# The second product of a squared-ReLU MLP: three of its four rounds by seven half-size products in place of eight

## The chip, the core and the metric

One Trainium2 chip, one of its cores. The metric is device time of one execution in microseconds (us). TensorE (PE) multiplies, VectorE (DVE) and ScalarE (ACT) do the elementwise work, GpSimd (POOL) some small parts, SyncE (SP) starts the transfers. The runs of the kernel before took 2602.18, 2602.62 and 2603.87 us.

## The reference

Four residual layers on 512 tokens of 1024 channels, float32. Layer i has a token mixer (retention in layers 0 and 3, a Conformer convolution in layer 1, a short gated convolution in layer 2) and then an MLP with 4096 hidden channels; each sublayer stands between two RMS norms.

```python
def squared_relu_mlp(x, w1, w2):
    return jnp.square(jax.nn.relu(x @ w1)) @ w2

    for i in range(DEPTH):
        ...
        x = x + rms_norm(h, norm_g[i, 1])
        h = squared_relu_mlp(rms_norm(x, norm_g[i, 2]), mlp_w1[i], mlp_w2[i])
        x = x + rms_norm(h, norm_g[i, 3])
```

## The kernel before, in words

Every float32 operand of a product is split into two float32r parts, the first part by ACT and the rest by DVE, and each product is three (`mm3`, lines 273 to 278): high by high, high by low, low by high. Weights come as pieces of 128x1024 (512 KB) in the order in which they are used (`piece_list`, line 64). `load` (line 214) starts the transfer of the next piece into one of two raw buffers, `fetch_hi` (L243) and `fetch_lo` (L250) split it into `whi` and `wlo`, of which there are `W_BUFS` = 8 of each. `settle` (line 260) splits one piece for each that has been used up, so pieces stand split some steps ahead.

All engines' orders are the order of the program: each engine takes its instructions one after the other. Only the conformer's part is ordered by a list schedule (`Plan`, line 128) with its own estimates of costs; `AHEAD` there is the number of pieces of the following product that it splits beforehand.

A sublayer begins with `first_four` (line 301): its first four channel tiles, of 128 channels, in two halves of the tokens, while the last token blocks are still normed, transposed (L393) and placed in `xin` (L324, L325). Then `tile` (line 292) makes one channel tile after the other, for all 512 tokens in one PSUM bank: 24 products of 512 columns (L286, L287, L289).

The MLP runs in four rounds q. In each, eight channel tiles of the first product come out of PSUM by relu (ACT, L1149), its square (DVE, L1150; ACT for the first part, L1151) and the second part (DVE, L1152) into two tiles `hid` of 4x512 columns. Then `out_round` (line 402) multiplies the 1024 hidden channels by eight pieces of the second weight matrix, token-major: two column halves, four pieces each, four token blocks in four banks (L276 to L278). The banks are copied to `f` (ACT, L417, first round) or added to it (DVE, L419). The last round is `out_final` (line 451), which also does the norm after the sublayer (`post_norm`, `add`, L368, L376), the norm before the next (`pre_sum`, `pre_norm`, L382), and the transposes. The residual stream `x` stays in SBUF through the MLP; only ahead of layer 3 it is parked in DRAM, since retention uses its place.

Of the kernel before, what the change touches and what calls it, by code (L numbers as in the profile page):

```python
# [16 lines left out]
P = 128  # L17
# [8 lines left out]
W_BUFS = 8  # L26
# [3 lines left out]
# the depthwise convolution: its channel tiles that run on the tensor engine as products of two  # L30
# token phases with pieces of 8 taps, and how many taps of each other tile the Pool engine adds up
# [5 lines left out]
AHEAD = 8  # L37
# [9 lines left out]
# columns of the per-partition parameter array  # L47
# [16 lines left out]
def piece_list():  # L64
    """The weight pieces in the order in which the kernel consumes them."""
# [10 lines left out]
    for layer in LAYERS:  # L76
# [44 lines left out]
        for q in range(4):  # L121
            for ft in range(8):
                ws("mlp_w1", layer, 8 * q + ft)
            ts("mlp_w2", layer, range(4 * q, 4 * q + 4))
# [3 lines left out]
class Plan:  # L128
    """Orders jobs of several engines by a list schedule and issues them in that order."""
# [10 lines left out]
    def run(self):  # L140
# [12 lines left out]
        while todo:  # L153
# [10 lines left out]
            # a more important job that is about to be ready goes first  # L164
# [12 lines left out]
class Trunk:  # L177
    def __init__(self, tc, wall, x_in, pos, norm_g, small, bpw2, decay, out):
# [3 lines left out]
        self.pieces = piece_list()  # L182
        self.issued = self.from_wall = self.loaded = self.used = self.owed = 0
# [30 lines left out]
    def load(self):  # L214
        """Starts the transfer of the next piece."""
# [4 lines left out]
        if self.pieces[i][0] == "phase":  # L220
            return self.load()
# [8 lines left out]
    def fetch_hi(self):  # L230
        """The first float32r part of the next piece."""
# [7 lines left out]
        if kind == "phase":  # L239
# [5 lines left out]
    def fetch_lo(self, i):  # L245
        """The second part."""
        nc = self.nc
        hi, lo = self.ready[i]
        if self.pieces[i][0] != "phase":
            nc.vector.tensor_sub(lo, self.raws.pop(i), hi.bitcast(F32))  # L250
            if i > 3:
                self.load()

# [6 lines left out]
    def settle(self, most=99):  # L260
        """Splits a piece for each one that has been used up."""
        while self.owed and most and not self.planned:
# [29 lines left out]
    def tile(self):  # L292
        """The next channel tile of a product, for all tokens."""
# [33 lines left out]
    def high(self, hi, lo, val):  # L327
        """The first part now, the second with the next call or with flush()."""
# [21 lines left out]
    def begin_boundary(self, post, pre):  # L350
        """Tiles for the end of one sublayer and the start of the next."""
# [50 lines left out]
    def out_round(self, slots, first):  # L402
        """One round of 8 contraction tiles that is not the last; adds into f."""
# [31 lines left out]
    def ts_part(self, banks, piece, slots, kp, late=False):  # L435
        """late: the second parts of slots come later than the first."""
# [137 lines left out]
    def retention(self, layer, first):  # L574
# [14 lines left out]

        def rope(banks, which):  # L590
            b1, b2 = banks
            for half in range(2):
# [9 lines left out]
                # the last block of keys meets only its own queries: it stays float32  # L602
# [167 lines left out]
    def newton(self, v, r0, t, eps):  # L770
        """-2/sqrt(v + eps) by one Newton step from the table's value r0; t holds its square."""
# [6 lines left out]
    def build_phases(self):  # L778
        """The matrices of the convolution's taps for POLY, in float32r parts, to DRAM.

        Rows (s, ch), columns (k, p, ch'): the tap 2k + s - p of channel ch, where ch = ch'."""
        nc = self.nc
        n = 64 * len(POLY)
        taps = self.mix.tile([P, 2, n], F32R, tag="st", bufs=1, name="taps")
        mask = self.mix.tile([P, 64], F32, tag="slast", bufs=1, name="mask")
# [65 lines left out]
        # the order of the tensor engine  # L851
# [282 lines left out]
    def mlp(self, layer, first):  # L1134
        nc = self.nc

        src = self.tiles(first)
        for q in range(4):
            slots = []
            for ft in range(8):  # L1140
                bank = next(src)
                if layer + 1 < DEPTH and mixer_of(layer + 1) == 1:
                    for _ in range(2 if ft == 7 else 1):
# [256 lines left out]
```

## Time and profile before

| | before |
|---|---|
| median of three runs | 2602.62 us (2602.18 to 2603.87) |
| profiled execution | span 2600.4 us from its first to its last instruction; the start and end around it have no time of their own on the page |
| instructions | 30770 |
| DVE, ACT, POOL busy | 1344.6 us (52%), 1011.5 us (39%), 213.1 us (8%) |
| HBM read, written | 256.88 MB, 12.58 MB |

The profile is taken in one execution of the program. "Busy" adds the lengths of an engine's instructions, overlaps counted once; for PE, products overlap in the pipe, so the spacing of their starts, not their length, tells how fast they go. Idle time of an engine counts only where another waits for it.

### The profile page before, as it was taken

How to read it: one execution, taken by the hardware profiler on the slowest of the kernel's cores; microseconds unless marked ns; L12 is line 12 of the kernel's file. 1: busy time of each engine (PE TensorE's matmuls, PEld its weight loads, DVE VectorE, ACT ScalarE, POOL GpSimd, SP SyncE). 2: the span in 40 equal slices, each digit the busy share in tenths (PEclk: the TensorE clock that was granted, in tenths of full speed). 3: DMA queues.
4: the chain of work that ended last, by engine and by line, in shares of the span. 5: the costliest groups of instructions: out<-in, count | busy, mean ns of one | idle time of the engine just before them, and what ended most of it. 6: DMA issues, size and time to landing. Idle time of an engine off the chain costs nothing. (4 is left out here: it accounts for less than half of the span.)

```text
span 2600.4 us, 30770 instructions
## 1 busy us (share of the span) xinstructions
PE 2577.7 (99%) x12461; PEld 2175.4 (84%) x12461; DVE 1344.6 (52%) x1615; ACT 1011.5 (39%) x1485; POOL 213.1 (8%) x248
## 2 busy tenths in 40 slices
PE   9999999999999999999999999999999999999998
PEld 8888888888888788888888888888888888888887
DVE  7654347345458973343464453343746534634433
ACT  4543445323236653322332343223444344433321
POOL 1000001000018710000010100000100000100000
PEclk9999999999999999999999999999999999999999
DMA  4333233334323433222322232223322323222221
GB/s 157 101 98 105 81 130 111 116 124 134 120 79 124 162 114 114 97 91 97 105 98 98 81 122 97 97 98 114 118 85 86 101 81 124 96 97 97 98 98 57
DMA packets 79838, 273.10 MB, mean 105 GB/s; under 512 B 8912, under 2 KB 10704, under 8 KB 79696
## 3 DMA queue, kind: packets, MB, share of 16 engines
q1 hardware_dynamic: 79696, 271.13, 31.0%
q8 instruction: 98, 1.61, 0.3%
q14 instruction: 44, 0.36, 0.0%
HBM read 256.88 MB, written 12.58 MB: 104 GB/s over the span
## 5 line engine op out<-in xcount | busy, mean ns | idle before, releaser
L250 DVE TENSOR_TENSOR wlo<-raw,whi 128x1024 fp32r<-128x1024 f32 x436 | 537.1, 1234 | 671.0 <-ACT whi L243 655.1
L286 PE MATMUL bank<-xin,whi 128*128 128x512 f32 (+1 forms) x2112 | 752.4, 365 | 0.2 <-ACT xin L324 0.2
L287 PE MATMUL bank<-xin,wlo 128*128 128x512 f32 (+1 forms) x2112 | 749.5, 363 | 0.0
L243 ACT ACTIVATE whi<-raw 128x1024 fp32r<-128x1024 f32 x436 | 457.7, 1053 | 627.3 <-PE bank L278 524.5
L289 PE MATMUL bank<-xin,whi 128*128 128x512 f32 (+1 forms) x2112 | 472.9, 364 | 3.7 <-DVE xin L325 3.7
L286 PEld LDWEIGHTS bank<-xin,whi 128*128 128x128 f32 x2112 | 398.3, 189 | 62.7 <-ACT xin L324 0.5
L287 PEld LDWEIGHTS bank<-xin,wlo 128*128 128x128 f32 x2112 | 398.5, 189 | 62.3
L289 PEld LDWEIGHTS bank<-xin,whi 128*128 128x128 f32 x2112 | 368.4, 189 | 67.7 <-DVE xin L325 5.4
L276 PE MATMUL bank<-whi,hid 128*128 128x512 f32 (+1 forms) x1032 | 400.3, 388 | 0.0
L278 PE MATMUL bank<-whi,hid 128*128 128x512 f32 (+1 forms) x1032 | 399.8, 387 | 0.0
L277 PE MATMUL bank<-wlo,hid 128*128 128x512 f32 (+1 forms) x1032 | 399.8, 387 | 0.0
L1150 DVE SCALAR_TENSOR_TENSOR tmp<-bank,tmp 128x512 f32<-128x512 f32 x128 | 88.4, 691 | 282.1 <-ACT tmp L1149 282.1
L278 PEld LDWEIGHTS bank<-whi,hid 128*128 128x128 f32 x1032 | 193.8, 188 | 39.7
L276 PEld LDWEIGHTS bank<-whi,hid 128*128 128x128 f32 x1032 | 193.8, 188 | 39.6
L277 PEld LDWEIGHTS bank<-wlo,hid 128*128 128x128 f32 x1032 | 193.8, 188 | 39.2
L1149 ACT ACTIVATE tmp<-bank 128x512 f32<-128x512 f32 x128 | 76.4, 597 | 374.1 <-PE bank L289 374.1
L344 POOL TENSOR_SCALAR tiny<-tiny,tiny 128x1 f32<-128x1 f32 x32 | 52.4, 1637 | 1550.9 <-ACT tmp L363 1549.7
L1010 POOL TENSOR_TENSOR pbuf<-pbuf 128x512 f32<-128x512 f32 x69 | 99.6, 1458 | 17.3 <-DMA raw<-wall 14.1
L276 PE MATMUL bank<-whi,y 128*128 128x512 f32 x256 | 99.9, 390 | 0.0
L278 PE MATMUL bank<-whi,y 128*128 128x512 f32 x256 | 99.6, 389 | 0.0
L276 PE MATMUL bank<-whi,xin 128*128 128x512 f32 x256 | 99.6, 389 | 0.0
L277 PE MATMUL bank<-wlo,xin 128*128 128x512 f32 x256 | 99.6, 389 | 0.0
(180 smaller groups left out, 2522.8 us busy)
## 6 DMA issues: line engine op xcount, KB each, us to landing
raw<-wall SPq DMA_DIRECT2D x436, 512.0 KB, 3.2
bnd<-norm_g SPq DMA_DIRECT2D x16, 512.0 KB, 6.4
phase<-tmp SPq DMA_DIRECT2D x32, 256.0 KB, 3.9
x<-x_in SPq DMA_DIRECT2D x8, 512.0 KB, 6.2
whi<-phase SPq DMA_DIRECT2D x8, 512.0 KB, 6.8
wlo<-phase SPq DMA_DIRECT2D x8, 512.0 KB, 8.3
early<-wall SPq DMA_DIRECT2D x4, 512.0 KB, 8.8
dec<-decay SPq DMA_DIRECT2D x8, 256.0 KB, 2.7
```

The costliest lines, as they stand in the source:

```text
L243: nc.scalar.activation(hi, self.raws[i], AF.Copy)
L250: nc.vector.tensor_sub(lo, self.raws.pop(i), hi.bitcast(F32))
L276: nc.tensor.matmul(out, ah, bh, start=start, stop=False)
L277: nc.tensor.matmul(out, ah, bl, start=False, stop=False)
L278: nc.tensor.matmul(out, al, bh, start=False, stop=stop)
L286: self.nc.tensor.matmul(out, wh[:, c], x, start=kt == 0, stop=False)
L287: self.nc.tensor.matmul(out, wl[:, c], x, start=False, stop=False)
L289: self.nc.tensor.matmul(out, wh[:, kt * P:(kt + 1) * P], self.xin[:, 1, kt, t0:t1], start=False, stop=kt == 7)
L344: nc.gpsimd.tensor_scalar(ms, parts[0], parts[1], EPS, op0=ALU.add, op1=ALU.add)
L1010: nc.gpsimd.tensor_tensor(accs[c], accs[c], pbuf[:, slot, :], op=ALU.add)
L1149: nc.scalar.activation(r, bank, AF.Relu)
L1150: nc.vector.scalar_tensor_tensor(s, bank, 0.0, r, op0=ALU.max, op1=ALU.mult)
```

## The change

In the first three rounds of each MLP (`FAST` = 3) the second product is done by Strassen's algorithm in the form of Winograd. The 512 tokens, the 1024 hidden channels and the 1024 output channels are halved each, so that there are four blocks of hidden values (two token halves `near[0]` and `near[1]`, the four even tiles `a` and the four odd tiles `b` in the order `PAIRED`) and four blocks of weights. Seven sums or differences of blocks ("forms") are multiplied, in the order `FORMS`, in place of eight products of blocks, and `takers` says to which quarters of `f` each form's result is added or from which it is subtracted.

What follows from this in the code:

- The hidden values: relu and square on ACT, then per pair of tiles four additions or subtractions of 256 columns on DVE (`s14`, `s23`), and splits into the tiles `own`, `far`, `mid`, `end`. `mid` takes the place of the residual `x`, which each mixer's `out_final` now stores to DRAM (`park`), and which is read back in the fourth round.
- The weights: the eight pieces of a round are loaded unsplit into eight blocks `blk` (`load_block`); a form's two pieces are made of them in place by `combine` (DVE) for forms 5, 6, 7 and 4, and split like a piece (14 for 8). In round 0 the eight loads start together after the MLP's first tile; in rounds 1 and 2 one with each piece of the first product.
- The sums: a form has two banks; each goes to one or two quarters of `f` (20 additions of 512 columns per round for 8, in round 0 eight of them as copies on ACT). `fast_end` makes two late sums in the fourth round.
- Room: `W_BUFS` and `AHEAD` are 7 for 8. `first_four` first splits pieces until four are ready. The rotary tables are stored to DRAM in layer 0 and read back in layer 3.

PE's list has 10,301 rows before and 10,013 now. The core of the diff:

```diff
-W_BUFS = 8
+W_BUFS = 7
-AHEAD = 8
+AHEAD = 7
+FAST = 3
+FORMS = (1, 2, 5, 6, 3, 7, 4)
+PAIRED = (0, 4, 1, 5, 2, 6, 3, 7)
...
     def fetch_lo(self, i):
...
+        if kind == "fast":
+            self.combine(*self.pieces[i + 1])
+            nc.vector.tensor_sub(lo, self.form_of(c, n), hi.bitcast(F32))
...
+            if name == "mlp_w1" and 1 <= c // 8 < FAST:
+                self.load_block(idx, c // 8, PAIRED.index(c % 8))
...
+        a, b = {5: ((0, 1), (0, 0)), 6: ((1, 1), (0, 0)), 7: ((1, 1), (0, 1)), 4: ((1, 0), (0, 0))}[form]
+        self.nc.vector.tensor_sub(self.form_of(form, g), self.blk[(g, *a)], self.blk[(g, *b)])
...
     def first_four(self, start):
+        self.settle(4 - len(self.ready))
         pieces = self.use(4)
...
+        def hidden():
+            bank = next(src)
+            s = self.tmp()
+            nc.scalar.activation(s, bank, AF.Relu)
+            nc.scalar.activation(s, s, AF.Square)
+            return s
...
+        for q in range(FAST):
...
+            for i in range(4):
+                a = hidden()
+                if q == 0 and i == 0:
...
+                    for n in range(8):
+                        self.load_block(layer, 0, n)
+                self.split(own[:, 0, i, near[0]], own[:, 1, i, near[0]], a[:, near[0]])
+                build(False)
+                b = hidden()
+                self.split(far[:, 0, i, :], far[:, 1, i, :], b)
...
+                nc.vector.tensor_add(s14[:, near[0]], a[:, near[1]], b[:, near[1]])
+                nc.vector.tensor_sub(s23[:, near[0]], s14[:, near[0]], a[:, near[0]])
+                nc.vector.tensor_sub(s23[:, near[1]], a[:, near[0]], a[:, near[1]])
+                nc.vector.tensor_sub(s14[:, near[1]], b[:, near[0]], s23[:, near[0]])
+                self.split(own[:, 0, i, near[1]], own[:, 1, i, near[1]], s14[:, near[0]])
+                self.split(mid[:, 0, i, :], mid[:, 1, i, :], s23)
+                self.split(end[:, 0, i, :], end[:, 1, i, :], s14[:, near[1]])
+                build(i == 3)
...
+    def fast_round(self, left, first):
...
+        takers = {1: ((0, 0, 1), (1, 1, 1)), 2: ((0, 0, 1),), 5: ((1, 1, 1), (1, 0, -1)), 6: ((1, 1, 1),),
+                  3: ((0, 1, 1),), 7: ((1, 1, 1), (0, 1, -1)), 4: ((1, 0, 1),)}
+        for form in FORMS:
+            banks = [self.bank(), self.bank()]
+            tile, t0 = left[form]
+            for g in range(2):
+                self.settle()
+                (piece,) = self.use()
+                for j in range(2):
+                    k = 2 * g + j
+                    for n, bank in enumerate(banks):
+                        c = slice(t0 + n * P, t0 + (n + 1) * P)
+                        self.mm3(bank, (tile[:, 0, k, c], tile[:, 1, k, c]), self.rhs(piece, j), k == 0, k == 3)
+                self.owed += 1
+            for n, bank in enumerate(banks):
+                for m, d, sign in takers[form]:
...
+            def park(b):
+                nc.sync.dma_start(self.x_park[b], self.x[:, b, :])
...
-                    first = self.out_final(slots, mode, None)
+                first = self.out_final(slots, mode, park)
```

DVE's order at the boundary of layer 0's mixer and MLP, before: the add of token block 3, a piece's second part, the placing of block 2, the norm of block 3, and the placing of block 3.

```order
L376 SCALAR_TENSOR_TENSOR x_2941<-f_2047,tiny_3280,x_2941 128x1024
L250 TENSOR_TENSOR wlo_3336<-raw_3048,whi_3335 128x1024
L325 TENSOR_TENSOR xin_2949<-bank_3325,xin_2949 128x4x128
L325 TENSOR_TENSOR xin_2949<-bank_3330,xin_2949 128x4x128
L382 SCALAR_TENSOR_TENSOR bnd_2946<-x_2941,tiny_3348,bnd_2946 128x1024
L250 TENSOR_TENSOR wlo_3353<-raw_3078,whi_3352 128x1024
L325 TENSOR_TENSOR xin_2949<-bank_3406,xin_2949 128x4x128
L325 TENSOR_TENSOR xin_2949<-bank_3411,xin_2949 128x4x128
L250 TENSOR_TENSOR wlo_3433<-raw_3339,whi_3432 128x1024
```

The same place after the change (L428 is the add, L282 the second part of a piece, L377 the placing, L434 the norm):

```order
L428 SCALAR_TENSOR_TENSOR x_2939<-f_2045,tiny_3282,x_2939 128x1024
L282 TENSOR_TENSOR wlo_3294<-raw_3047,whi_3293 128x1024
L282 TENSOR_TENSOR wlo_3350<-raw_3077,whi_3349 128x1024
L377 TENSOR_TENSOR xin_2948<-bank_3339,xin_2948 128x4x128
L377 TENSOR_TENSOR xin_2948<-bank_3344,xin_2948 128x4x128
L434 SCALAR_TENSOR_TENSOR bnd_2945<-x_2939,tiny_3362,bnd_2945 128x1024
L282 TENSOR_TENSOR wlo_3367<-raw_3297,whi_3366 128x1024
L377 TENSOR_TENSOR xin_2948<-bank_3420,xin_2948 128x4x128
L377 TENSOR_TENSOR xin_2948<-bank_3425,xin_2948 128x4x128
L282 TENSOR_TENSOR wlo_3447<-raw_3353,whi_3446 128x1024
```

One more second part of a piece (`wlo`) stands between the add of block 3 and the placing of block 2, ahead of the norm of block 3 (`bnd`).

DVE's order in the second product, round 1 of layer 0, before: second parts of pieces, and after four of them the additions of four banks into `f`.

```order
L250 TENSOR_TENSOR wlo_4355<-raw_4271,whi_4354 128x1024
L250 TENSOR_TENSOR wlo_4385<-raw_4311,whi_4384 128x1024
L250 TENSOR_TENSOR wlo_4415<-raw_4358,whi_4414 128x1024
L250 TENSOR_TENSOR wlo_4445<-raw_4388,whi_4444 128x1024
L419 TENSOR_TENSOR f_3764<-f_3764,bank_4350 128x512
L419 TENSOR_TENSOR f_3764<-f_3764,bank_4351 128x512
L419 TENSOR_TENSOR f_3764<-f_3764,bank_4352 128x512
L419 TENSOR_TENSOR f_3764<-f_3764,bank_4353 128x512
```

Round 1 of layer 0 after the change, from the first form on (`blk` are weight blocks; L303 is `combine`, L280 the second part of a form's piece):

```order
L1287 TENSOR_TENSOR f_3816<-f_3816,bank_4462 128x512 x2
L1287 TENSOR_TENSOR f_3816<-f_3816,bank_4463 128x512 x2
L280 TENSOR_TENSOR wlo_4504<-blk_3483,whi_4503 128x1024
L303 TENSOR_TENSOR blk_3482<-blk_3483,blk_3482 128x1024
L280 TENSOR_TENSOR wlo_4520<-blk_3479,whi_4519 128x1024
L1287 TENSOR_TENSOR f_3816<-f_3816,bank_4501 128x512
L1287 TENSOR_TENSOR f_3816<-f_3816,bank_4502 128x512
L303 TENSOR_TENSOR blk_3479<-blk_3479 128x1024
L280 TENSOR_TENSOR wlo_4541<-blk_3482,whi_4540 128x1024
L303 TENSOR_TENSOR blk_3481<-blk_3481,blk_3480 128x1024
L280 TENSOR_TENSOR wlo_4558<-blk_3479,whi_4557 128x1024
L1287 TENSOR_TENSOR f_3816<-f_3816,bank_4538 128x512
```

Between two forms' additions stand two second parts and up to two combinations, where eight additions and eight second parts made up the round before.

## Rows read from the trace of the kernel before

**Rows 1.** The page: busy time of each engine; granted clock in 40 slices.

```profile
PE 2577.7 (99%) x12461; PEld 2175.4 (84%) x12461; DVE 1344.6 (52%) x1615; ACT 1011.5 (39%) x1485; POOL 213.1 (8%) x248
...
PEclk9999999999999999999999999999999999999999
```

**Rows 2.** Stretches of layer 3's MLP: length, busy us (instructions) by engine, clock, DMA.

```profile
2331.78:2375.30 43.52, 43.52 (x193) 36.04 (x193) 19.50 (x22) 16.81 (x23) 0.00 (x0) 1.00 0.28 91
2375.30:2418.82 43.52, 43.52 (x193) 36.04 (x193) 15.64 (x17) 9.61 (x10) 0.00 (x0) 1.00 0.30 103
```

**Rows 3.** Groups of instructions: line, engine, tiles, shapes, count | busy us, mean ns | idle.

```profile
L276 PE MATMUL bank<-whi,hid 128*128 128x512 f32 x1016 | 395.7, 390 | 0.0
L250 DVE TENSOR_TENSOR wlo<-raw,whi 128x1024 fp32r<-128x1024 f32 x436 | 537.1, 1234 | 671.0 <-ACT whi L243 655.1
L243 ACT ACTIVATE whi<-raw 128x1024 fp32r<-128x1024 f32 x436 | 457.7, 1053 | 627.3 <-PE bank L278 524.5 <-DMA raw<-wall 65.1 <-PE bank L289 29.8
L1151 ACT ACTIVATE hid<-tmp 128x512 fp32r<-128x512 f32 x128 | 81.0, 633 | 4.1
L419 DVE TENSOR_TENSOR f<-f,bank 128x512 f32<-128x512 f32 x64 | 42.5, 684 | 19.8 <-PE bank L278 19.8
L337 DVE TENSOR_TENSOR st<-tmp,st 128x256 fp32r<-128x256 f32 x8 | 3.4, 426 | 0.2
```

**Rows 4.** Timeline of DVE, layer 3's MLP: start us, length us, instruction [idle before].

```profile
2257.52 1.23 DVE L250 TENSOR_TENSOR wlo<-raw,whi 128x1024 fp32r<-128x1024 f32 x1 [1.10 <-ACT whi L243]
2258.66 0.69 DVE L1150 SCALAR_TENSOR_TENSOR tmp<-bank,tmp 128x512 f32<-128x512 f32 x1
2259.45 0.69 DVE L1152 TENSOR_TENSOR hid<-tmp,hid 128x512 fp32r<-128x512 f32 x1
...
2393.89 1.28 DVE L419 TENSOR_TENSOR f<-f,bank 128x512 f32<-128x512 f32 x2
```

**Rows 5.** Timeline of DVE, boundary of layer 3's mixer and MLP.

```profile
2247.12 1.28 DVE L376 SCALAR_TENSOR_TENSOR x<-f,tiny,x 128x1024 f32<-128x1024 f32 x1 [0.77 <-POOL tiny L347]
...
2250.66 1.27 DVE L382 SCALAR_TENSOR_TENSOR bnd<-x,tiny,bnd 128x1024 f32<-128x1024 f32 x1
...
2253.76 1.29 DVE L325 TENSOR_TENSOR xin<-bank,xin 128x512 fp32r<-128x512 f32 x2 [0.69 <-ACT xin L324]
```

**Rows 6.** Timeline of ACT, the same boundary.

```profile
2253.13 1.09 ACT L324 ACTIVATE xin<-bank 128x512 fp32r<-128x512 f32 x2 [2.58 <-PE bank L393]
```

**Rows 7.** Timeline of PE, first transposes of all; then the same boundary.

```profile
9.53 2.29 PE L393 MATMUL bank<-ident,bnd 128*128 128x128 f32 x16 [1.40 <-DVE bnd L382]
...
2250.57 0.64 PE L289 MATMUL bank<-xin,whi 128*128 128x256 f32 x4
...
2252.01 0.64 PE L289 MATMUL bank<-xin,whi 128*128 128x256 f32 x4
2252.49 1.03 PE L393 MATMUL bank<-ident,bnd 128*128 128x128 f32 x8
```

**Rows 8.** PE's waits: line waited for: us in total, times, longest us.

```profile
PE bank L914 <- DVE conv L990: 4.4, 2, 3.5
PE bank L393 <- DVE bnd L382: 4.1, 3, 1.6
PE bank L289 <- DVE xin L325: 3.7, 8, 0.9
```

**Rows 9.** DMA issues: count, KB, median us to landing; a stretch of the start (last: GB/s).

```profile
raw<-wall SPq DMA_DIRECT2D x436, 512.0 KB, 3.2
early<-wall SPq DMA_DIRECT2D x4, 512.0 KB, 8.8
park<-x SPq DMA_DIRECT2D x4, 512.0 KB, 2.7
...
2.10:16.00 13.90, 11.77 (x82) 10.90 (x81) 7.68 (x9) 8.47 (x14) 2.93 (x6) 1.00 0.97 370
```

More of the change, by code (lines that the diff above doesn't have):

```diff
@@ L121, in piece_list, with blocks, wall_list @@
         for q in range(4):
-            for ft in range(8):
+            for ft in PAIRED if q < FAST else range(8):
                 ws("mlp_w1", layer, 8 * q + ft)
-            ts("mlp_w2", layer, range(4 * q, 4 * q + 4))
+            if q < FAST:
+                out.extend(("fast", layer, q, form, g) for form in FORMS for g in range(2))
+            else:
+                ts("mlp_w2", layer, range(4 * q, 4 * q + 4))
+    return out
+def blocks(q):
+    return [((g, r, c), (4 * q + 2 * r + g, c)) for r, c in ((0, 0), (1, 0), (0, 1), (1, 1)) for g in range(2)]
+def wall_list():
+    out = [p for p in piece_list() if p[0] in ("ws", "ts")]
+    for layer in LAYERS:
+        for q in range(FAST):
+            out += [("ts", "mlp_w2", layer, *where) for _, where in blocks(q)]
     return out
@@ L219, in load @@
         self.issued += 1
-        if self.pieces[i][0] == "phase":
+        if self.pieces[i][0] not in ("ws", "ts"):
             return self.load()
@@ L260, in settle @@
     def settle(self, most=99):
-        while self.owed and most and not self.planned:
+        while self.owed and most > 0 and not self.planned:
             self.fetch()
@@ L588, in retention @@
         nc.vector.tensor_copy(ones, one)
+        if layer:
+            self.cos, self.sin = (rp.tile([P, S], F32, tag=n, bufs=1, name=self.nm(n)) for n in ("cos", "sin"))
+            for there, here in zip(self.angles, (self.cos, self.sin)):
+                nc.sync.dma_start(here, there)
         def rope(banks, which):
@@ L1137, in mlp @@
         src = self.tiles(first)
[L1138 to L1143, printed above, removed]
-                        next(self.building, None)
-                if ft % 4 == 0:
-                    slots.append(self.big.tile([P, 2, 4, S], F32R, tag="h", bufs=2, name=self.nm("hid")))
-                hh, hl = slots[-1][:, 0, ft % 4, :], slots[-1][:, 1, ft % 4, :]
-                r, s = self.tmp(), self.tmp()
-                nc.scalar.activation(r, bank, AF.Relu)
-                nc.vector.scalar_tensor_tensor(s, bank, 0.0, r, op0=ALU.max, op1=ALU.mult)
-                nc.scalar.activation(hh, r, AF.Square)
-                nc.vector.tensor_sub(hl, s, hh.bitcast(F32))
-            if q < 3:
-                self.out_round(slots, q == 0)
@@ new lines, in mlp @@
+        slots = []
+        for ft in range(8):
+            a = hidden()
+            if ft % 4 == 0:
+                slots.append(self.big.tile([P, 2, 4, S], F32R, tag="h", bufs=2, name=self.nm("hid")))
+            self.split(slots[-1][:, 0, ft % 4, :], slots[-1][:, 1, ft % 4, :], a)
+            if ft == 0:
+                self.x = self.big.tile([P, 4, D], F32, tag="x", name=self.nm("x"))
+            if 0 < ft < 5:
+                nc.sync.dma_start(self.x[:, ft - 1, :], self.x_park[ft - 1])
+            if ft in (3, 5):
+                self.fast_end(ft // 2 - 1)
+            build(ft == 7)
@@ new lines, in mlp @@
+        return slots, "add"
+    def fast_round(self, left, first):
+        nc = self.nc
+        if first:
+            self.f = self.big.tile([P, 4, D], F32, tag="f", name=self.nm("f"))
+        takers = {1: ((0, 0, 1), (1, 1, 1)), 2: ((0, 0, 1),), 5: ((1, 1, 1), (1, 0, -1)), 6: ((1, 1, 1),),
+                  3: ((0, 1, 1),), 7: ((1, 1, 1), (0, 1, -1)), 4: ((1, 0, 1),)}
+        seen = set()
+        for form in FORMS:
[12 more added lines that the diff above has]
+                for m, d, sign in takers[form]:
+                    f = self.f[:, 2 * m + n, d * 512:(d + 1) * 512]
+                    if first and (m, d) not in seen:
+                        nc.scalar.activation(f, bank, AF.Copy, scale=float(sign))
+                    elif sign > 0:
+                        nc.vector.tensor_add(f, f, bank)
+                    else:
+                        nc.vector.tensor_sub(f, f, bank)
+            seen.update((m, d) for m, d, _ in takers[form])
@@ L1218, in rotary @@
         nc.scalar.activation(self.cos, t, AF.Sin, scale=-1.0, bias=self.half_pi)
+        for there, here in zip(self.angles, (self.cos, self.sin)):
+            nc.sync.dma_start(there, here)
         yield
@@ L1235, in build @@
             self.x_park = [dram.tile([P, D], F32, name=f"park{b}") for b in range(4)]
+            self.angles = [dram.tile([P, S], F32, name=f"angle{n}") for n in range(2)]
             self.neg_half = self.const(-0.5, "neg_half")
@@ L1294, in begin @@
                 banks = [next(f)]
-                for _ in range(3):
+                for _ in range(W_BUFS - 5):
                     next(turn)
                     self.fetch()
-                next(turn)
+                for _ in range(9 - W_BUFS):
+                    next(turn)
                 next(turn)
@@ L1316, in build @@
                 self.begin_boundary((layer, 3), self.next_pre)
-                store = None
-                if not last and mixer_of(layer + 1) == 0:
-                    store = lambda b: nc.sync.dma_start(self.x_park[b], self.x[:, b, :])
-                first = self.out_final(slots, mode, store)
+                back = not last and mixer_of(layer + 1) == 0
+                first = self.out_final(slots, mode, park if back else None)
 def decay_tables():
@@ L1345, in tile_of @@
         return t[i] if form == "ws" else t[i, c]
-    pieces = [p for p in piece_list() if p[0] != "phase"]
+    pieces = wall_list()
     wall = np.empty((len(pieces), P, D), np.float32)
```

55 lines of the change are left out of this document (47 added, 8 removed).

## The prediction

> **What bounds the kernel now.** I read the page's busy times first: the tensor engine (PE) is busy for 2577.7 of 2600.4 us, at its higher clock level throughout (2.4 GHz, granted clock in tenths 9 in all 40 slices) [rows 1]. So the time is the number of products times their spacing, plus some 23 us in which PE has nothing to do. Next I cut one MLP into stretches: eight tiles of the first product take 43.52 us, and so does one old round of the second product, and in both PE is busy to the last hundredth [rows 2]. 192 products of 512 columns stand in each (the count of 193 includes one cut by the edge): 43.52 / 192 = 0.2267 us from one to the next, 5.44 us for the 24 of one tile. The 390 ns that the groups give for one product [rows 3] is its length in the pipe, not its spacing, and isn't used. VectorE (DVE) is busy 19.50 us in the first of these stretches and 15.64 us in the second, ScalarE (ACT) 16.81 and 9.61 [rows 2]: both have more than half of the time free. PE's own waits are short and lie at the sublayer boundaries and in the conformer [rows 8].
>
> **The products.** An old round is 2 column halves x 4 pieces x 4 token blocks x 2 x 3 = 192 products. A new one is 7 forms x 2 pieces x 2 x 2 token blocks x 3 = 168, of the same 128x128 weights and 512 columns. That is 24 fewer, 24 x 0.2267 = 5.44 us; with 3 rounds in each of 4 layers 288 products and **65.3 us**. PE's order confirms the count: 10,301 rows before, 10,013 now. The products sit in stretches where PE never waits, so each one left out shortens the path, if the other engines keep up.
>
> By the Trainium skill (TensorE: Matmul & The Clock Gate, Part 1) a warm product starts N / 2.4 GHz + 2.5 ns after the one before, 215.7 ns for 512 columns. The rows say 226.7 ns, so the trace doesn't agree; by the page's figure the gain would be 288 x 0.2157 = 62.1 us and the time about 3 us above my forecast.
>
> **DVE in a new round.** The spacing counts here, not the length: a subtraction of 1024 columns starts at 2257.52 and the next instruction at 2258.66, 1.14 us; one that needs the result before it takes 0.79 us at 512 columns (2258.66 to 2259.45); two additions out of PSUM take 1.28 us together, so 1.28 - 0.68 = 0.60 us each [rows 3, 4]. For 256 columns I take the mean of one, 0.43 us [rows 3], and 0.10 us for each being dependent (0.79 - 0.69): 0.53 us. A round with its eight tiles then has on DVE: 8 + 14 second parts of weight pieces and 8 combinations of weight blocks, 30 x 1.14 = 34.2; 20 additions into f, 20 x 0.60 = 12.0; and for each of four pairs of tiles 7 of 256 columns and 2 of 512, 7 x 0.53 + 2 x 0.60 = 4.9, together 19.6. Sum 65.8 us, against 8 x 5.44 + 38.1 = 81.6 us of PE. In layer 0 the matrices for the convolution add nine instructions of 512 columns, about 0.69 us each, 72.0 us. ACT has 22 first parts at 1.05 = 23.1 [rows 3], 16 passes over banks and squares at 0.63 = 10.1, and five splits per pair, at most 0.63 each, 12.6: 45.8 us. So neither becomes the bound on average.
>
> The densest place is the first four forms: 8 second parts, 5 combinations, 12 additions, 13 x 1.14 + 12 x 0.60 = 22.0 us beside 4 x 5.44 = 21.8 us of PE. DVE enters it late, by the chain behind the last tile (relu and square 1.26, then a first part, a second part, four adds, the remaining parts: some 5.5 us), and leaves it some 5.7 us late. What may it be late? A piece is split six pieces ahead of its use (7 buffers), and a piece is now 12 products, 2.72 us: 16.3 us. In PSUM, four forms of two banks each fill the 8 banks, so an addition has three forms, 16.3 us, too. Margin about 10 us: I cost the work on DVE and ACT at nothing, hidden by PE's products. If this cover is gone, a round costs what DVE's sum exceeds 81.6 by.
>
> **Block loads.** Rounds 1 and 2 load one block per first-product tile, the bytes of before at their old pace. Round 0 sends eight at once, 4 MB, behind the first tile of the MLP. At the start, 13.9 us moved 370 GB/s [rows 9], so 4 MB need some 11 us. The first form's product is eight tiles, more than 33 us, away. ACT and DVE may stand for some us behind such a load (in layer 0 also behind a small load for the taps that is queued after the blocks); PE then has its pieces and banks for several tiles. Cost nothing.
>
> **Boundaries.** This is where the 7 buffers cost. Before, four pieces were split when the next sublayer began; now three are, and the fourth is split after the add of token block 3 and before the placing of block 2. DVE's row shows what stands behind: add at 2247.12, one split, two placings, the norm of block 3 from 2250.66 to 2251.93 [rows 5]; PE's transposes of that block began at 2252.49 [rows 7]. Slack 0.56 us; the extra 1.14 us pushes the norm to 2253.07, and PE waits 0.58 us. At two boundaries PE already waits there (of three waits, together 4.1 us, the longest 1.6, one of 1.40 is at the start) [rows 7, 8]: there the whole 1.14 counts. Seven boundaries: 5 x 0.58 + 2 x 1.14 = 5.2 us.
> The second thing there: two raw buffers serve the first two splits, and now a third split, ahead of block 3's placing on ACT, needs a transfer that starts only when the first is done, about 2249.5. It lands 3.2 us later (median) [rows 9], 2252.7, splits until 2253.8; ACT's placing stood at 2253.13 after 2.58 us of idle [rows 6] and now begins about 2253.8. PE's work between, transposes (about 1.0) and one eighth (1.44) [rows 7], runs to about 2255.5, so placing until 2254.9 is in time. At the four boundaries with a parked residual, the store of block 3 (2.7 us to land) runs just ahead of that transfer and can make it later: between 0 and 1.5 us each; I take 0.25, because the slack of 0.6 us swallows most: 1.0 us. Sum for boundaries **6.2 us**, with 0 and 14 us as the ends (14: 7 x 1.14 + 4 x 1.5).
>
> **The rest.** The reload of the residual is in the last quarter, ahead of its use by tiles: nothing. Reloaded rotary tables: two transfers of 256 KB at the start of layer 3, and two stores in layer 0 that SP issues once the sine is there; raw loads behind them have a lead of pieces: nothing. In the conformer the planner orders the same work with one buffer fewer. PE's order there has the same products, DVE's taps move by a place or two; PE waits 4.4 us for DVE there [rows 8], which may grow or shrink by one second part either way, -1 to +2 us; I take 0.
>
> **Sum.** 2600.4 - 65.3 + 6.2 = 2541.3 for the span. The median of the three runs, 2602.62, lies 2.2 us above the span; I keep these: **2543.5 us**. What the measurement can tell from no change is about 0.2%, 5 us.
>
> **Rivals.**
> *DVE runs late in the rounds (chance 0.12).* For it: in rounds of layer 0, 72.0 of 81.6 us, and each second part needs ACT's first part; at boundaries such partners let DVE idle by 0.6 to 0.7 us (0.69 before the placing, [rows 5]). If each of the 22 second parts paid 0.6 us, +13 us: 79 us in most layers, 85 in layer 0. Then layer 0 loses 3 x 3.5 us and the densest stretches of the other nine rounds perhaps 1 us: 20 us, 2563. Against it: first parts run well ahead, since ACT has little else to do in a round.
> *The boundaries cost nothing (0.06)*: 2537. The norm's slack could be larger where PE arrives later.
> *Slower than before (0.03).* The eight block loads of round 0 come one after the other at the 8.8 us that transfers took to land when many were queued at the start [rows 9]. Eight are 70.4 us, and combining and splitting 3.5 more, 73.9; PE asks for the eighth block's first piece after 8 tiles and 7 pieces less the part of the first tile, about 33 + 19 = 52 us. Wait 22 us in each of 4 layers, 88 us: 2543.5 + 88 = 2631. It turns to slower when a layer waits over 59 / 4 = 15 us, that is over 8 us a block. Against: 8.8 us is the time in a queue with others, and the window of 370 GB/s shows 1.4 us per block.
> That the change does less than it says can't be: the products are counted.
>
> **How the numbers follow.** Forecast 0.79, its own range 2537 to 2552 (boundaries 0 to 14). DVE late 0.12, no boundary cost 0.06, slower 0.03. The range of 8 in 10 takes the forecast's ends and reaches to the DVE rival: 2536 to 2562. Faster by over 0.2% holds in all but the last and small part of the DVE case: 0.95; within 0.2% 0.02; slower 0.03.
>
> **What would show it.** Products in a new round: 168 in 38.1 us with PE busy throughout; PE's span of an MLP shorter by 16.3 us. PE waiting for the norm of block 3 (transposes) some 0.6 us more at each boundary, and for nothing in the rounds. DVE busy 60 to 70 us of each 81.6. The forecast is wrong if PE's list of waits names weight pieces or banks inside the rounds, if products come slower than 0.2267 us there, or if ACT's wait for block loads reaches PE in round 0.

## The result, and the profile after

The changed kernel takes 2545.99 us (median; 2543.64 to 2547.59) where the kernel before takes 2602.49 in the same session (2602.18 to 2603.87): 0.9781 of it, 95% interval 0.9768 to 0.9795. The forecast was 2543.5 in a range of 2536 to 2562: the direction and nearly all of the size are right, and the time is 2.5 us above it. The profiled execution has a span of 2544.1 us, 56.3 less than before.

The page of the changed kernel, busy times and granted clock:

```profile
PE 2516.4 (99%) x12173; PEld 2124.6 (84%) x12173; DVE 1652.9 (65%) x2151; ACT 1210.3 (48%) x1829; POOL 218.4 (9%) x248
...
PEclk9999999999999999999999999999999999999999
```

Against [rows 1] PE has exactly 288 products fewer, but is busy 61.3 us less, not 65.3; its idle time (span less busy) rose from 22.7 to 27.7 us. So 56.3 = 65.3 - 5.0 of new idle time - 4.0 of longer busy time: products at the lower clock (some 3.4 us more than before, below), and the ends of products ahead of new stops. A 512-column product that nothing follows counts as busy for its whole 0.39 us, where the next one would have started after 0.23. DVE has 308 us more, ACT 199.

Windows of layer 3's second round, as [rows 2]: first the eight tiles, then the seven forms.

```profile
2286.37:2329.89 43.52, 43.52 (x194) 36.04 (x193) 30.11 (x46) 25.76 (x40) 0.00 (x0) 1.00 0.33 122
2329.89:2367.97 38.08, 38.08 (x170) 31.53 (x169) 31.17 (x39) 15.40 (x18) 0.00 (x0) 1.00 0.20 72
```

The round is 5.44 us shorter and PE is busy to the hundredth. 38.08 us for 168 products is 0.2267 us each (the two more counted are cut by the edges). The forms take 38.08 us in all twelve rounds of the changed kernel but the first of layer 0 (38.69).

Where PE waits, as [rows 8] (L445 was L393, L971 was L914, L340 was L289):

```profile
PE bank L445 <- DVE bnd L434: 8.2, 8, 2.5
PE bank L971 <- DVE conv L1047: 4.3, 1, 4.3
PE bank L340 <- DVE xin L377: 3.2, 8, 0.9
PE bank L337 <- ACT xin L376: 2.3, 2, 2.0
PE bank L237 <- POOL ident masks.py:199: 1.3, 1, 1.3
PE bank L498 <- ACT z L1144: 0.9, 1, 0.9
PE bank L329 <- DVE own L377: 0.3, 1, 0.3
```

Two lines matter. The transposes (L445) wait at all seven boundaries and at the start, 4.1 us more in all (3.5 at the boundaries; the wait at the start is anything from 0.7 to 1.9 us in the kernels of this study); and a wait of 2.0 us for a placing (L337 behind ACT) is new. The first two boundaries' transposes:

```profile
424.09 1.06 PE L445 MATMUL bank<-ident,bnd 128*128 128x128 f32 x8 [0.56 <-DVE bnd L434]
764.65 1.06 PE L445 MATMUL bank<-ident,bnd 128*128 128x128 f32 x8 [2.49 <-DVE bnd L434]
```

In the rounds PE waits 0.3 us in the whole program (`own`, layer 0), and the round there is 0.6 us longer than the others.

The new wait stands at the boundary between layer 2's MLP and layer 3's retention. ACT's timeline there, SP's, and PE's (start, length, instruction, idle before):

```profile
1811.76 1.06 ACT L271 ACTIVATE whi<-raw 128x1024 fp32r<-128x1024 f32 x1 [6.95 <-DMA raw<-wall]
1812.72 1.07 ACT L376 ACTIVATE xin<-bank 128x512 fp32r<-128x512 f32 x2
```

```profile
1803.66 0.32 SPq L1447 DMA_DIRECT2D park<-x  x1
1804.03 0.42 SPq L645 DMA_DIRECT2D cos<-angle  x1
1804.49 0.78 SPq L645 DMA_DIRECT2D sin<-angle  x1
1805.32 0.50 SPq L704 DMA_DIRECT2D dec<-decay  x1
1805.91 8.52 SPq L252 DMA_DIRECT2D raw<-wall  x3
```

```profile
1808.84 1.06 PE L445 MATMUL bank<-ident,bnd 128*128 128x128 f32 x8 [0.96 <-DVE bnd L434]
...
1813.36 0.39 PE L337 MATMUL bank<-xin,whi 128*128 128x256 f32 x1 [2.02 <-ACT xin L376]
...
1815.43 0.41 PE L337 MATMUL bank<-xin,whi 128*128 128x256 f32 x1
1815.65 0.41 PE L338 MATMUL bank<-xin,wlo 128*128 128x256 f32 x1
```

The reloads of the two rotary tables stand on SP ahead of the raw pieces; ACT, which must split one of these before it places block 3, stands idle for 6.95 us, and PE for 2.02. Behind that wait the products come at 0.22 us where they came at 0.12 for the same 256 columns. The windows show why (columns as in [rows 2], the granted clock stands third from the end):

```profile
1814.00:1816.00 2.00, 2.00 (x14) 2.00 (x14) 2.00 (x4) 0.74 (x1) 0.00 (x0) 0.68 0.45 125
1816.00:1818.00 2.00, 2.00 (x12) 2.00 (x11) 0.41 (x1) 0.20 (x1) 0.00 (x0) 0.50 0.63 203
1818.00:1820.00 2.00, 2.00 (x18) 2.00 (x18) 1.10 (x1) 0.86 (x1) 0.00 (x0) 0.96 0.49 197
```

A little over a microsecond after that wait the granted clock fell to 0.50, the lower level of 1.2 GHz, and it stayed there for some 3.4 us: 2 x (0.32 + 0.50 + 0.04) = 1.7 us of work lost, nearly as much as the wait.

### The profile page after: what moved, and what is told of

It reads as the page before. It is cut to its first block, busy times and chain, and to the rows that moved or that the text cites. A ratio compares the mean times of both kernels' runs of the same rounds, so it can differ in the third digit from the quotient of the medians.

```text
span 2544.1 us, 30985 instructions
## 1 busy us (share of the span) xinstructions
PE 2516.4 (99%) x12173; PEld 2124.6 (84%) x12173; DVE 1652.9 (65%) x2151; ACT 1210.3 (48%) x1829; POOL 218.4 (9%) x248
## 5 line engine op out<-in xcount | busy, mean ns | idle before, releaser
L337 PE MATMUL bank<-xin,whi 128*128 128x512 f32 (+1 forms) x2112 | 753.3, 365 | 2.3 <-ACT xin L376 2.3
L282 DVE TENSOR_TENSOR wlo<-raw,whi 128x1024 fp32r<-128x1024 f32 x340 | 416.8, 1234 | 426.5 <-ACT whi L271 425.2
L271 ACT ACTIVATE whi<-raw 128x1024 fp32r<-128x1024 f32 x340 | 354.8, 1053 | 428.9 <-DMA raw<-wall 214.7
L340 PE MATMUL bank<-xin,whi 128*128 128x512 f32 (+1 forms) x2112 | 473.8, 364 | 3.2 <-DVE xin L377 3.2
L337 PEld LDWEIGHTS bank<-xin,whi 128*128 128x128 f32 x2112 | 398.9, 189 | 65.0 <-ACT xin L376 2.9
L340 PEld LDWEIGHTS bank<-xin,whi 128*128 128x128 f32 x2112 | 369.3, 189 | 67.1 <-DVE xin L377 4.8
L266 ACT ACTIVATE whi<-blk 128x1024 fp32r<-128x1024 f32 x168 | 174.5, 1053 | 123.1 <-DVE blk L303 117.0
L280 DVE TENSOR_TENSOR wlo<-blk,whi 128x1024 fp32r<-128x1024 f32 x168 | 204.8, 1221 | 19.9 <-ACT whi L266 18.7
L1287 DVE TENSOR_TENSOR f<-f,bank 128x512 f32<-128x512 f32 x168 | 108.4, 681 | 0.0
L327 PE MATMUL bank<-whi,hid 128*128 128x512 f32 (+1 forms) x264 | 101.5, 385 | 0.0
L329 PE MATMUL bank<-whi,hid 128*128 128x512 f32 (+1 forms) x264 | 101.0, 383 | 0.0
L328 PE MATMUL bank<-wlo,hid 128*128 128x512 f32 (+1 forms) x264 | 101.0, 383 | 0.0
L328 PE MATMUL bank<-wlo,y 128*128 128x512 f32 x256 | 99.6, 389 | 0.0
```

The lines of the kernel that those rows point to most:

```text
L266: nc.scalar.activation(hi, self.form_of(c, n), AF.Copy)
L271: nc.scalar.activation(hi, self.raws[i], AF.Copy)
L280: nc.vector.tensor_sub(lo, self.form_of(c, n), hi.bitcast(F32))
L327: nc.tensor.matmul(out, ah, bh, start=start, stop=False)
L328: nc.tensor.matmul(out, ah, bl, start=False, stop=False)
L329: nc.tensor.matmul(out, al, bh, start=False, stop=stop)
```

## The experiments

Each edit is one to the changed kernel unless something else is said. "Theory" is the forecast's: the products give 65.3 us, the boundaries take some back, and the rest is hidden. All times are medians; the kernel before took 2603.2 in the session of the first four, 2603.1 in that of the next four, and 2602.3 in that of the last two. The changed kernel's 2545.99 is from the session of the result, where the kernel before took 2602.49; a difference to it of about 1 us between sessions shows nothing.

**The two halves of the change apart.** First, all the new surroundings (seven split pieces, parking, tables), with rounds of eight products:

```diff
-FAST = 3
+FAST = 0
...
+        for q in range(3):
+            slots = []
+            for ft in range(8):
...
+            self.out_round(slots, q == 0)
```

> All that surrounds the change stays (seven buffers, parked residual, stored rotary tables, squares on ACT), but the first three rounds are done by eight products of blocks again, as before the change. Theory (the forms' side work on DVE, ACT and the queues is hidden, so the forms are worth their 288 products at 0.2267 us, 65.3 us, less 0.3 to 0.7 us of waits in layer 0): 2546.0 + 65.0 = 2611.0 us, within 1. Rival (the side work costs some of it in waits at other places, 4 us or more): 2607 us or less.

Measured: 2607.96 us (2607.40 to 2610.01), 1.0020 of before (1.0011 to 1.0029). The surroundings cost about 5 us and the products give 2607.96 - 2545.99 = 62.0, between the 65.0 of the theory and the rival's 61 or less. Its page and its waits:

```profile
PE 2580.3 (99%) x12461; PEld 2177.9 (84%) x12461; DVE 1254.4 (48%) x1487; ACT 1092.8 (42%) x1613; POOL 218.7 (8%) x248
```

```profile
PE bank L445 <- DVE bnd L434: 7.2, 8, 2.5
...
PE bank L337 <- ACT xin L376: 1.7, 2, 1.4
```

Against the changed kernel PE is busy 63.9 us more and idle 1.8 us less. What is missing to 65.3 lies for the most part outside the rounds. From the first to the last product of the second weight matrix, PE takes 306.20 us here, as before the change, in each of layers 0 to 2 and 304.83 in layer 3; in the changed kernel it is 16.32 us less in each of layers 1 to 3, which is three times 5.44, and 15.71 less in layer 0: 64.7 us in all. The wait at the tables is 1.4 us here and no fall of the clock follows it; with the new rounds it is 2.0 and 1.7 more follow. Why it is 0.6 us longer with them no run shows.

Then the kernel before with nothing but seven split pieces (`begin`, at the start of the program, follows the number):

```diff
-W_BUFS = 8
+W_BUFS = 7
-AHEAD = 8
+AHEAD = 7
...
     def first_four(self, start):
+        self.settle(4 - len(self.ready))
```

> The kernel before with seven buffers for eight (and the split of pieces at a sublayer's start until four are ready), nothing parked more than before. Theory: the extra split ahead of block 3's norm makes PE wait 0.56 us at five boundaries and some 0.9 more into the conformer, and in layer 3's start the raw piece comes behind one parked block alone: 2602.5 + 4 = 2606.5 us, with waits of the transposes of about 8 us. Rival (the parked residual makes those waits): 2602.5 us, waits of the transposes 4.1 us as before.

Measured: 2607.03 us (2605.58 to 2608.64), 1.0015 (1.0006 to 1.0024): 3.9 us more than the kernel before in the same session, where the theory had 4. Its first wait:

```profile
PE bank L394 <- DVE bnd L383: 8.1, 8, 2.5
```

These are the waits of the changed kernel, at the same places and within 0.02 us of the same length at each boundary, though no more is parked here than before. The cost of the boundaries is that of seven buffers in place of eight; the parking adds nothing to these waits. The conformer's wait in one piece (4.3 us) comes with seven buffers too.

**The boundaries.** The fourth piece is split just ahead of the first product that needs it:

```diff
     def first_four(self, start):
-        self.settle(4 - len(self.ready))
-        pieces = self.use(4)
+        pieces = self.use(3)
...
+            if i == 6:
+                pieces += self.use(1)
```

> The changed kernel, but a sublayer's fourth weight piece is taken only ahead of its use in the seventh eighth of the first half, so no extra split stands ahead of the norm of token block 3, and no third raw transfer ahead of the placing of block 3. Theory (the seven buffers cost at the boundaries, by that split and that transfer): the transposes' waits of 0.56 us go at five boundaries (2.8 us), the one of 2.5 us falls to 1.6 (0.9), and at the boundary into layer 3's retention the wait of 0.96, the 2.02 us for the placing and the stretch at the lower clock level behind it (about 1.7 us) go (4.7): 8.3 us in all, 2537.7 us. Rival (the boundaries wait because of the parked residual's stores, or because all engines come later there): the waits stay, 2545 to 2547 us.

Measured: 2540.26 us (2538.98 to 2541.11), 0.9758 (0.9745 to 0.9772). The waits for the norm are gone but at the start and ahead of the conformer (1.5 each), and so is the wait at the tables. What is missing of the expected gain is in two places, layer 0's first round (`own`) and the conformer, whose wait is 5.3 us where the changed kernel has 4.3:

```profile
PE bank L972 <- DVE conv L1048: 5.3, 1, 5.3
...
PE bank L446 <- DVE bnd L435: 3.0, 2, 1.5
PE bank L327 <- ACT own L377: 1.8, 1, 1.8
...
PE bank L329 <- DVE own L378: 0.7, 1, 0.7
```

In layer 0 ACT waited 9.03 us for the small load of the taps, behind the blocks. From 465 to 470 us, behind PE's waits there, the granted clock was 0.66.

The tables of layer 3 loaded after the first channel tile there, alone:

```diff
-        if layer:
-            self.cos, self.sin = (rp.tile(...) for n in ("cos", "sin"))
-            for there, here in zip(self.angles, (self.cos, self.sin)):
-                nc.sync.dma_start(here, there)
...
-                rope([next(src), next(src)], which)
+                pair = [next(src)]
+                if tables and which == 0:
...
+                        nc.sync.dma_start(here, there)
+                rope(pair + [next(src)], which)
```

> The changed kernel, but the two rotary tables of layer 3 are loaded after its first channel tile, not ahead of everything at its start. Theory (in layer 3's start the tables' 512 KB stand ahead of the raw piece for which ACT waits, and the placing of block 3 is queued behind that wait): the 2.02 us wait and the lower clock behind it go, 0.96 falls to 0.56: 4.1 us, 2541.9 us, and the retention doesn't wait for its tables on PE. Rival (the parked residual's store alone makes that raw piece late): the wait stays within 0.5 us, 2545.5 us.

Measured: 2543.73 us (2542.92 to 2544.31), 0.9771 (0.9758 to 0.9785): 2.3 us of the expected 4. The wait for the placing fell from 2.3 to 0.6 us and the clock stayed at 1.00 there, so the tables were a cause of both. It takes them and the third split together: with the fourth piece split late and the tables left where they were, and with seven pieces alone, the wait is not there either. In the profiled execution the rest was given back ahead of the conformer, where the same wait of 2.5 us as in the changed kernel was followed by a stretch at the lower clock (below). The 2.3 us are the medians' difference between two sessions, and the changed kernel's own four runs spread over 4 us, so how much of the expected 4 came is not shown; the waits are.

Both edits, and the taps' load issued ahead of the first blocks (`build` issues it and is called ahead of the MLP's first tile):

```diff
         near = slice(0, 256), slice(256, 512)
+        build(False)
...
-                build(i == 3)
+                build(i == 3 and q > 0)
```

> The late fourth piece and the late rotary tables together, and the small load of the convolution's taps in layer 0 is started ahead of the MLP's first tile, so that it isn't queued behind the eight weight blocks. Theory (ACT stands some 9 us behind that load, and this makes the first form's left operand late by 2.5 us in layer 0, with a lower clock behind it): against the late fourth piece alone 2.5 us of waits and 1 us of clock less: 2540.3 - 3.5 = 2536.8 us; PE has no wait for the tile own. Rival (ACT is late there for its own work, not for that load): 2540 us, the wait stays.

Measured: **2536.08 us** (2535.85 to 2536.57), 0.9743 (0.9729 to 0.9758), 10 us better than the changed kernel and the best of all. Its waits, all of them:

```profile
PE bank L973 <- DVE conv L1049: 5.3, 1, 5.3
PE bank L340 <- DVE xin L378: 3.1, 8, 0.9
PE bank L446 <- DVE bnd L435: 2.6, 2, 1.6
PE bank L237 <- POOL ident masks.py:199: 1.3, 1, 1.3
PE bank L499 <- ACT z L1146: 0.9, 1, 0.9
PE bank L337 <- ACT xin L377: 0.2, 1, 0.2
```

Retention, the rounds and six of the seven boundaries have no wait over 0.9 us. From the first to the last product of the second weight matrix, all four layers now take 16.32 us less than before the change: 65.3 us together.

**DVE's margin.** Behind each form's products, ahead of its sums, two spare additions (a tile of its own, read by nobody else):

```diff
+            for _ in range(2):
+                nc.vector.tensor_add(self.spare, self.spare, self.spare)
             for n, bank in enumerate(banks):
```

> The changed kernel with two extra additions of 512 columns on DVE behind each form (a spare tile that nobody reads; 14 a round, each dependent on the one before, 0.79 us: 11.1 us a round). Theory (DVE may be 16.3 us late in a round; it leaves the densest four forms 6.0 us late): 6.0 + 8 x 0.79 = 12.3 us, under 16.3, and 62 + 11 = 73 us of 81.6 a round: no new wait in PE's rounds, 2546 us, at most 2 more. Rival (the cover ends earlier than worked out, DVE's lateness reaches PE already): 2556 us or more.

Measured: 2552.23 us (2551.17 to 2553.49), 0.9804 (0.9787 to 0.9820), 6.2 more than the changed kernel: between the two expectations. With four in place of two:

> The same with four extra additions behind each form (22.1 us a round). Theory: lateness 6.0 + 16 x 0.79 = 18.6 us, over 16.3, and 62.2 + 22.1 = 84.3 us of DVE for 81.6 of PE, 90.5 in layer 0 with the matrices for the convolution, about 5 less in each round 0: 6 rounds of 2.7 us, and in layer 0 two of 8.9 and one of 4.1: 38 us, 2584 us, with PE waiting inside the rounds for DVE's second parts or sums. Rival (ACT and the loads slow DVE too, or the cover is much larger): outside 2570 to 2600 us.

Measured: 2614.12 us (2612.92 to 2616.84), 1.0044 (1.0029 to 1.0059), 68 more: far from the 38 expected. Windows of the forms' products of one round, DVE third. With two additions, layer 0's second round and layer 1's:

```profile
542.41:582.25 39.84, 38.38 (x170) 31.46 (x168) 39.52 (x52) 15.89 (x21) 0.00 (x0) 1.00 0.07 27
1076.11:1114.19 38.08, 38.08 (x170) 31.53 (x168) 35.53 (x47) 13.49 (x17) 0.00 (x0) 1.00 0.07 24
```

With four, layer 3's first round and its second:

```profile
2302.38:2340.45 38.07, 38.07 (x169) 31.53 (x168) 34.92 (x46) 17.16 (x24) 0.00 (x0) 1.00 0.01 1
2383.97:2428.25 44.28, 40.54 (x170) 32.54 (x168) 43.68 (x58) 16.69 (x22) 0.00 (x0) 0.96 0.00 1
```

In the rows with DVE busy for less than the 38.08 us of the forms (31.17 in the changed kernel, 34.92 and 35.53 here), PE loses nothing; where DVE has more, PE waits for second parts of weight pieces, and for sums that have to free a bank. With two additions that is so only in layer 0, whose rounds also build the matrices for the convolution: 1.8 us lost in the second round (DVE 39.52) and 3.3 in the third (40.77). With four it is so in layer 0 (8 to 10 us a round) and in every second and third round of the others (6.2 to 7.5): 6.2 us in the row above, of which 3.7 are waits and 1.7 the granted clock of 0.96. Its waits:

```profile
PE bank L328 <- DVE wlo L280: 32.1, 17, 2.9
PE bank L445 <- DVE bnd L434: 10.0, 8, 2.5
PE bank L327 <- DVE f L1293: 5.7, 7, 0.8
```

Its nine long rounds together are 67.8 us over 38.08 each, so nearly all of the loss lies in the forms' stretches. Over the whole program 42.6 of the 67.8 us that its span is longer are idle time of PE, and 25.2 are longer busy time, which my 38 left out: some 19 by the granted clock (in windows of 5 us); of the other 6 a part is the ends of products ahead of the stops, as in the changed kernel, and the rest isn't placed. My 38 also spread DVE's work over tiles and forms together, where only the forms' stretch decides.

**The block loads.** Each of the eight loads of round 0 is issued twice:

```diff
-                    for n in range(8):
-                        self.load_block(layer, 0, n)
+                    for n in range(16):
+                        self.load_block(layer, 0, n // 2)
```

> The changed kernel with each of the eight block loads of round 0 done twice (8 MB in place of 4, in every layer). Theory (4 MB more at about 370 GB/s are 11 us; PE asks for the blocks only after eight tiles, so in layers 1 to 3 nothing reaches it; in layer 0 the small load of the taps stands behind them, ACT behind that load, and the left operands of the first form, already 0.3 us late, come up to 11 us later): 2546 + 11 = 2557 us, with PE's wait for the tile own in layer 0 alone. Rival of the slower side (block loads come one after the other slowly enough to reach PE in every layer): 2546 + 4 x 11 = 2590 us, with waits for weight pieces. A third outcome, 2546 us, would say that the loads reach PE nowhere.

Measured: 2575.08 us (2574.64 to 2575.98), 0.9893 (0.9879 to 0.9908): 29 more, and neither theory's number. Its waits, SP's timeline and ACT's in layer 0:

```profile
PE bank L327 <- ACT whi L266: 12.2, 1, 12.2
PE bank L327 <- ACT own L376: 11.4, 3, 5.6
```

```profile
428.39 38.05 SPq L291 DMA_DIRECT2D blk<-wall  x16
466.49 0.43 SPq L845 DMA_DIRECT2D tmp<-small  x1
```

```profile
469.65 0.31 ACT L376 ACTIVATE taps<-tmp 128x128 fp32r<-128x128 f32 x1 [33.61 <-DMA tmp<-small]
```

SP issues the load for the taps behind all the blocks, 38 us later. ACT, whose order has their split early in the first round, stands for 33.61 us, with everything for PE queued behind it. All of the two long waits but 1.8 us (layer 3) is in layer 0, where the clock also was at 0.50 to 0.84 from 460 to 495 us. In the changed kernel the same wait of ACT is 6.5 us, and PE had enough pieces to wait only 0.3. To tell the taps from the blocks, the taps' load went ahead of them, alone and with the blocks doubled:

> One change to the changed kernel: in layer 0 the load of the taps' weights is issued ahead of the first block loads instead of behind them. In the profile of the changed kernel PE waits only 0.3 us for the operand that hangs on it, so both theories expect nearly no change: 2545.0 to 2546.5 us. A rival in which the block loads ahead of the taps already cost the changed kernel something that its waits do not show: 2542 us or less.

> The same kernel with each block of round 0 loaded twice. Theory: the 29 us that doubling cost before were the taps' load, queued behind 38 us of block loads in layer 0, with ScalarE's queue standing behind it (waits of 12.2 and 11.4 us there, plus the stretches at the lower clock after them); with the taps ahead, the doubled blocks cost only the 1.8 us wait in layer 3 and what the clock adds to it: 2546 to 2550 us. Rival: the blocks themselves come too late: 2565 us or more, with waits for the blocks in layer 0.

Measured: 2544.72 us (2543.71 to 2546.80), 0.9778 (0.9762 to 0.9795), no change to the changed kernel; and with the doubled blocks 2551.59 (2550.94 to 2553.13), 0.9805 (0.9790 to 0.9819). So of the 29 us that doubling cost, 6.9 are the blocks themselves (2551.59 - 2544.72, one session) and the other 22 were the taps' load behind them. The waits of the doubled kernel that are left are a little more than I expected (2546 to 2550):

```profile
PE bank L327 <- ACT own L376: 2.3, 2, 1.9
PE bank L328 <- DVE wlo L280: 2.2, 1, 2.2
```

The eight blocks as they are, then, hide completely: with the taps' load moved, PE has no wait in any round. Doubled to 8 MB, they just begin to show.

## Why the prediction was right, and where it was off

- **Bound and products: right.** 288 products fewer, 0.2267 us each, PE busy throughout in the rounds: in layers 1 to 3 the second product shrank by 16.32 us where 16.3 was forecast, in layer 0 by 15.71. The figure of the Trainium skill (TensorE: Matmul & The Clock Gate, Part 1) gives 62.1 as an estimate; the rounds show 5.44 us each, so the trace decides. That the rounds brought 62.0 net against rounds of eight has another cause, the waits and the clock, most of them outside the rounds.
- **DVE in a round: right that it hides, and near in size.** 61.3 us busy in the tiles and forms shown above (65.8 forecast), 68.7 in layer 0's second (72.0). The term that was too large is that of the pairs of tiles, 4.9 us each: their nine instructions take some 3.8 in the trace, since of those of 256 columns some are 0.46 apart and most 0.33 to 0.34, where 0.53 was taken for all. DVE came to its first forms' work 5.5 us late, as reckoned, and left the fourth 6.0 late (5.7). But the rule "a round costs what DVE's sum exceeds 81.6 by" was too mild: with four spare additions DVE was busy for 79.2 us in layer 3's second round, less than 81.6, and PE lost 6.2 us in it. The stretch that counts is the forms' own 38 us.
- **Block loads: right at nothing.** The serial rival can't hold: doubled, and with the taps ahead, they cost 6.9 us, where the rival had 88 for the eight alone. The small load behind them, which the forecast named and passed over, was the thin place: 0.3 us of wait here (0.6 in the round's length, and 38.08 us as in the others with that load alone moved), 1.8 and 0.7 and a fall of the clock as soon as something else moved, and 22 us with doubled blocks.
- **Boundaries: 6.2 us forecast; the transposes wait 3.5 us more there, and seven pieces in the kernel before cost 3.9 in all (1.6 to 6.2 by the interval).** The slack of 0.56 us was read right: at four of the seven boundaries PE waits 0.56 us where none was before (0.58 forecast). At the two where PE waited already, the whole 1.14 was wrong: ahead of the conformer 1.64 became 2.49, and behind it 1.07 became 0.56. The seventh, before layer 3's retention, waits 0.96. I have no row for why the wait behind the conformer went the other way. The third raw transfer and the store of block 3 were costed at 1.0; the store shows no wait of its own.
- **The step that failed: "Reloaded rotary tables ... raw loads behind them have a lead of pieces: nothing."** The lead is gone at just that place, since two raw buffers serve the first two splits and ACT must split a third piece ahead of the placing. The forecast had worked this out for the parked boundaries in the paragraph before, and didn't apply it to the two transfers that stand in the same queue. It cost 2.0 us of wait and 1.7 of clock; without the tables there both are gone.
- **The sum.** 2541.3 for the span was forecast, and 2544.1 measured: 2.8 more. That it came so near is in part luck, since the errors have both signs. Boundary waits took 2.7 us less than forecast; the tables took 3.7 more, and layer 0's first round 0.6. The conformer, forecast at 0, has its 4.3 us of waits for `conv` in one piece now, about as long as the two before, but the clock then loses 3.4 us for 1.7 before the change (by the granted clock in windows of 5 us). No term of the forecast held the clock, though it makes 3.4 of the 9.0 us by which the gain stays under 65.3. The forecast read the higher level as held throughout from tenths in 40 slices of 65 us; in windows of 5 us the kernel before shows 0.79 and 0.87 from 880 to 890 us.

## What to carry to other kernels

Where a matrix engine is busy without a gap, products left out are worth their spacing (16.32 us a layer here, forecast and measured), and the work that replaced them was free until DVE had more of it than the stretch in which it falls is long: compare the sums in that stretch, not over a period. Then look at what the surroundings lost to make room. Here one split buffer fewer and two reloads at the wrong place in a queue took back most of 9 us, and three moves of a few lines, none of which touches the products, won 10. A load that is small but queued behind big ones, and awaited by an engine whose other work feeds the bound one, belongs ahead of them.

## What the runs showed that was not expected

A wait of PE cost nearly its length again here, by the clock, or nothing. The wait of 2.5 us ahead of the conformer has the same length in nine kernels of this study. Windows of the 5 us behind it, first the changed kernel, then the one with later tables:

```profile
765.00:770.00 5.00, 5.00 (x45) 5.00 (x44) 3.49 (x4) 2.03 (x3) 0.00 (x0) 1.00 0.47 147
```

```profile
765.00:770.00 5.00, 5.00 (x32) 5.00 (x31) 3.71 (x4) 2.14 (x3) 0.00 (x0) 0.66 0.39 129
```

The clock stays at 1.00 in the one, as in the kernels with rounds of eight and with doubled blocks alone, and in the other it is 0.66, 1.7 us lost; as much is lost there with seven pieces alone, with two and with four spare additions, and with the taps' load moved (with the blocks doubled too). What decides between them no run here tells apart, and it need not be the edit: these are single executions, and the changed kernel's own runs go from 2543.64 us at a mean granted clock of 0.998 to 2547.59 at 0.996. Waits of 1.8 to 2.9 us were followed by a loss of 0 or 1.7 us nearly everywhere, and those of 3.5 to 5.3 us ahead of the conformer's `conv` products by 1.7 to 3.5. A forecast that prices waits by their length alone leaves this out.

A small load waited for the large ones issued just ahead of it: 64 KB for the taps landed 9.8 us after their issue behind eight blocks of 512 KB, where they took 3.1 us in the kernel before and 2.7 with the load moved ahead of the blocks.
